# A two-block transformer kernel: split products of 512 and 256 columns become three of 256, and the weights' parts move by 192 bytes

## The chip, the core and the metric

The kernel runs on one core of a Trainium2 chip. The metric is the device time of one execution in microseconds (us); the time shown for the kernel before is the median of three runs. The profile is one execution of the same program, taken by the hardware profiler. Engines are named as the profile names them: PE (TensorE matmuls), PEld (TensorE weight loads), DVE (VectorE), ACT (ScalarE), POOL (GpSimd) and SP (SyncE, which issues the transfers).

## What is computed

Two transformer blocks work on one sequence of 256 tokens with 2,048 features, all in float32. Cut to the products that matter here:

```python
# first block: gated convolution mixer, then an MLP of width 8192
h = rms_norm(x) * (1 + sc1) + sh1
a, gt = split(h @ conv_w_in + b_in)            # 2048 -> 4096
u = silu(layer_norm(conv31(a * sigmoid(gt))))
x = x + (1 + g1) * (u @ conv_w_out + b_out)
h = rms_norm(x) * (1 + sc2) + sh2
x = x + (1 + g2) * (square(relu(h @ mlp_w1)) @ mlp_w2)
# second block: two kinds of attention, merged under gates, then a gated MLP of width 5632
h = rms_norm(x) * (1 + sc1) + sh1
qa, ka, va, qb, kb, vb, ga, gb = split(h @ w_in)
merged = sigmoid(ga) * (attn_a @ w_oa) + sigmoid(gb) * (attn_b @ w_ob)
x = x + g1 * (merged @ w_out)
h2 = rms_norm(x) * (1 + sc2) + sh2
x = x + g2 * ((silu(h2 @ w_gate) * (h2 @ w_up)) @ w_down)
return rms_norm(x)
```

## The kernel before

**Split products.** Activations are kept transposed: 16 blocks of 128 features (`KB`) by 256 tokens (`S`). Every weight matrix is cut into 128 x 128 blocks. To keep float32 accuracy with the faster `float32r` matmul, each operand is split into a high part and a low part (the rest of the value): an activation block lies in SBUF as high and low part side by side, 2 x 256 columns (tiles `hHL`, `uHL` and `m`); a weight block is split into `wh` and `wl`. Of the four products three are taken: high weight by high activation, high weight by low activation, low weight by high activation. We call these three products of one 128 x 128 weight block a unit; a product with K = 2,048 has 16 units.

`mm` (lines 184 to 207) makes a unit of two matmuls. `main` (L191) puts `wh` through the array against all 512 columns, high and low part in one go, and writes the 512 columns of a PSUM bank. `corr` (L194) puts `wl` against the 256 high columns and adds to the first half of the bank. So a finished product lies in two halves, and `total` (L238) adds them: ACT copies the second half to SBUF (L243), DVE adds the first half to it (L246). In the last unit `corr` comes first and `main` last.

`mm_one` (L208, matmul at L210) makes the same unit of three matmuls of 256 columns, all into the first half of the bank; nothing has to be added behind it. Before the change it serves the products of the convolution mixer (L755, L759, L828). The first six pairs of those products (`early`, L573) are also made of three matmuls of 256 columns.

Every matmul is issued with its own weight load (LDWEIGHTS); the load of the next matmul runs while one streams.

**Order.** `linear` (L222) goes through the output blocks of a matrix: for each it takes the next weights (`take`, L160), makes the product (`mm_group`, L214) and evicts it through a function of the stage (`ev_up`, `partial`, `residual`, `ev_qkv`, `ev_ff`). `take` keeps one weight tile ahead: a 1 MB transfer into `wf` (L169), then for each half an ACT cast to `wh` (L177) and a DVE subtraction to `wl` (L180). Between the steps small jobs run that make the modulation vectors (L263, L265, L286) from weights of their own. The engines' instructions keep the order of the program.

**Addresses.** The `big` pool gives each tag one place, one behind the other: `uHL` (also `front`), `hHL`, then `a1` (16 columns, 64 bytes a partition), then `m` (also `slots`, `room`, `att` and the accumulators `ya`); the pools with `wf`, `wh`, `wl` and the small tiles follow behind. In bytes modulo 256, `hHL` and `uHL` begin at 224, `m` at 32, and every `wh` and `wl` at 96; each block inside them lies a multiple of 512 bytes further on. So an activation lies 128 bytes past its weights modulo 256 where it is read from `hHL` or `uHL`, and 192 bytes where it is read from `m`.

Of the kernel before, what the change touches and what calls it, by code (L numbers as in the profile page):

```python
# [11 lines left out]
AF = mybir.ActivationFunctionType  # L12
# [3 lines left out]
P = 128  # L16
D = 2048
KB = D // P
S = 256
# [53 lines left out]
class Builder:  # L73
# [110 lines left out]
    def mm(self, ps, w, k, x, first, last):  # L184

        wh, wl = w[k // 8]
        h, l = wh[:, k % 8, :], wl[:, k % 8, :]
        full = x.rearrange("p a t -> p (a t)")

        def main():  # L190
            self.nc.tensor.matmul(ps, lhsT=h, rhs=full, start=first, stop=last, skip_group_check=True)  # L191

        def corr():
            self.nc.tensor.matmul(ps[:, :S], lhsT=l, rhs=x[:, 0, :], start=False, stop=False, skip_group_check=True)  # L194

        if last:
            corr()
            main()
        else:
            main()  # L200
            corr()

    def mm_one(self, w, x, nk):

        ps = self.mmps()
        for k in range(nk):
            wh, wl = w[k // 8]
            h, l = wh[:, k % 8, :], wl[:, k % 8, :]  # L208
            for i, (a, b) in enumerate(((h, 0), (h, 1), (l, 0))):
                self.nc.tensor.matmul(ps[:, :S], lhsT=a, rhs=x[:, k, b], start=(k == 0 and i == 0),  # L210
                                      stop=(k == nk - 1 and i == 2))
        return ps

    def mm_group(self, ws, x, ks, xs=None):  # L214

        xs = xs or ks
        pss = [self.mmps() for _ in ws]
        for i, (k, kx) in enumerate(zip(ks, xs)):
            for ps, w in zip(pss, ws):
                self.mm(ps, w, k, x[:, kx], i == 0, i == len(ks) - 1)  # L220
        return pss

    def linear(self, n, x, nk, evict, step=None, lead=3):

        j = 0
        while j < n:
# [6 lines left out]
                if step:  # L233
                    step()
            j += g

    def total(self, ps, bias=None, out=None):

        nc = self.nc
        tb = self.t1()  # L240
        s = self.t1() if out is None else out
        if bias is None:
            nc.scalar.copy(tb, ps[:, S:])  # L243
        else:
            nc.scalar.activation(tb, ps[:, S:], AF.Identity, bias=bias)
        nc.vector.tensor_tensor(out=s, in0=ps[:, :S], in1=tb, op=ALU.add)  # L246
        return s


    def mod_part(self, src, part, cvec, bias, out):  # L250
# [207 lines left out]
    def build(self):  # L458
# [44 lines left out]
        front = self.big.tile([P, 2 * KB * S], F32, tag="uHL", name="front")  # L503
        xn = front[:, :KB * S].rearrange("p (k t) -> p k t", t=S)
        h = self.actHL("hHL")
        a1 = self.keep([P, 16], "a1")
        slots = self.big.tile([P, 4, D], F32, tag="m", name="slots")
        ring = [slots[:, n] for n in range(4)]
        ring += [front[:, KB * S + n * D:KB * S + (n + 1) * D] for n in range(RING - 4)]
# [237 lines left out]
        for i in range(EARLY, KB):  # L747
            sg = self.t1()
            if i in NATIVE:

                ps = self.mmps()
                for k in range(KB):
                    nc.tensor.matmul(ps[:, :S], lhsT=w[:, k], rhs=xn[:, k], start=(k == 0), stop=(k == KB - 1))  # L753
            else:
                ps = self.mm_one(w, h, KB)  # L755
            w = self.take()
            turn()
            nc.scalar.activation(sg, ps[:, :S], AF.Sigmoid, bias=self.vec("conv_b_in", i + 16))
            ps = self.mm_one(w, h, KB)  # L759
            if i < KB - 1:  # L760
                w = self.take()
            turn()
            glu(i, ps[:, :S], sg)
# [27 lines left out]
                                 bias=self.vec("conv_ln_b", kb))  # L791
            self.split(s[:, kb, 0], s[:, kb, 1], t)

        def residual(j, ps, g, stat=None, part=None):

            if stat is not None and j == KB - 1:
                src = x[:, j]
                if part is not None:
                    src = part[:, j]
                    nc.vector.scalar_tensor_tensor(out=src, in0=src, scalar=g[:, j:j + 1], in1=x[:, j],  # L800
                                                   op0=ALU.mult, op1=ALU.add)
                t = self.t1()
                nc.vector.scalar_tensor_tensor(out=t, in0=ps[:, S:], scalar=g[:, j:j + 1], in1=src,
                                               op0=ALU.mult, op1=ALU.add)
                nc.vector.scalar_tensor_tensor(out=x[:, j], in0=ps[:, :S], scalar=g[:, j:j + 1], in1=t,
                                               op0=ALU.mult, op1=ALU.add)
                self.square_sum(stat, x[:, j], j)
                return
            t = self.total(ps)
            if part is not None:  # L810
                nc.vector.tensor_tensor(out=t, in0=t, in1=part[:, j], op=ALU.add)
            nc.vector.scalar_tensor_tensor(out=x[:, j], in0=t, scalar=g[:, j:j + 1], in1=x[:, j],
                                           op0=ALU.mult, op1=ALU.add)
            if stat is not None:
                self.square_sum(stat, x[:, j], j)

        def partial(j, ps, part, first):
            if first:
                self.total(ps, out=part[:, j])
            else:  # L820
                t = self.total(ps)
                nc.vector.tensor_tensor(out=part[:, j], in0=part[:, j], in1=t, op=ALU.add)

        g1 = self.keep([P, 16], "g1")
        nc.vector.tensor_scalar_add(g1, mod(0, G1), 1.0)
        st = self.aux()
        for j in range(16):
            ps = self.mm_one(self.take(), s, KB)  # L828
            t = self.t1()
            nc.scalar.activation(t, ps[:, :S], AF.Identity, bias=self.vec("conv_b_out", j))  # L830
            nc.vector.scalar_tensor_tensor(out=x[:, j], in0=t, scalar=g1[:, j:j + 1], in1=x[:, j],
                                           op0=ALU.mult, op1=ALU.add)
            self.square_sum(st[:, :S], x[:, j], j)
            self.step()
# [12 lines left out]
        for g in range(4):  # L847
            u = self.actHL("uHL")

            def ev_up(j, ps, u=u):  # L850
                t, r, v = self.total(ps), self.t1(), self.t1()
                nc.scalar.activation(r, t, AF.Relu)
                nc.scalar.activation(v, r, AF.Square)
                self.split(u[:, j, 0], u[:, j, 1], v)

            self.linear(16, h, KB, ev_up, step=self.step,
                        lead=3 if g == 0 else 1)
            if g < 3:
                self.linear(16, u, KB, lambda j, ps, g=g: partial(j, ps, ya, g == 0), step=self.step, lead=1)
            else:  # L860
                self.flush()
                nc.vector.tensor_scalar_add(g2, mod(0, G2), 1.0)
                self.linear(16, u, KB, lambda j, ps: residual(j, ps, g2, st[:, :S], ya), lead=1)
# [43 lines left out]
        def ev_qkv(j, ps):  # L907
            blk = QKV_ORDER[j]
            new = None
            if blk < 10:  # L910
                t = qg[:, blk] if blk < 8 else kv[:, blk - 8]
                self.total(ps, out=t)
                new = self.head_norm_rope(t, self.vec("q_norm_w_2" if blk < 8 else "k_norm_w_2"))
            elif blk < 12:
                new = value(self.total(ps), kv[:, blk - 8])
            elif blk < 28:
                n, i = (blk - 12) // 8, (blk - 12) % 8
                self.total(ps, out=qk[:, i % 2, n])
                if n:
                    new = gqa(i)  # L920
            else:
                new = nat(self.total(ps), blk - 28)
            self.advance()
            if new is not None:
                self.stages.append(new)
# [7 lines left out]
        def gates(j):  # L933
            out = []
            for b in (36 + j, 52 + j):
                g = self.t1()
                nc.scalar.activation(g, self.total(self.mm_group([self.take()], h, list(range(16)))[0]),
                                     AF.Sigmoid)
                out.append(g)
                self.advance()  # L940
            return out

        nxt = gates(0)
        for j in range(16):
# [3 lines left out]
            while self.stages:  # L948
                self.advance()
            w = self.take()  # L950
            oa = self.total(self.mm_group([w], y, list(range(8)))[0])
            nc.vector.tensor_tensor(out=sa, in0=sa, in1=oa, op=ALU.mult)
            ob = self.total(self.mm_group([w], y, list(range(8, 16)))[0])
            nc.vector.tensor_tensor(out=sb, in0=sb, in1=ob, op=ALU.mult)
            nc.vector.tensor_tensor(out=sa, in0=sa, in1=sb, op=ALU.add)
            self.split(m[:, j, 0], m[:, j, 1], sa)
# [17 lines left out]
        for gi, n in enumerate(FF_GROUPS):  # L974
# [1 line left out]
            tmp = {}  # L976

            def ev_ff(j, ps, u=u, tmp=tmp):
                t = self.total(ps)
                if j % 2 == 0:  # L980
                    g = self.t1()
                    nc.scalar.activation(g, t, AF.Silu)
                    tmp[j] = g
                else:
                    g = tmp.pop(j - 1)
                    v = self.t1()
                    nc.vector.tensor_tensor(out=v, in0=t, in1=g, op=ALU.mult)
                    self.split(u[:, j // 2, 0], u[:, j // 2, 1], v)

            self.linear(2 * n, h, KB, ev_ff,  # L990
# [129 lines left out]
```

## Time and profile before

| | |
|---|---|
| median of three runs | 2594.88 us (2594.2 to 2595.09) |
| profiled execution, its own time | 2594.32 us |
| its span, first to last instruction | 2592.5 us |
| mean granted TensorE clock | 0.989 |
| PE busy | 2527.7 us, 97% of the span, 15340 matmuls |
| PEld busy | 2164.4 us, 83% |
| DVE busy | 1828.1 us, 71% |
| ACT busy | 1323.5 us, 51% |
| moved by DMA | 638.43 MB, mean 246 GB/s |

Busy time is the time in which an engine had an instruction under way; matmuls overlap each other in the pipeline, so for PE the starts of successive matmuls tell more than the busy time does. The timeline view lists instructions by their start; the view of one source line gives the shortest, the median and the longest duration of its instructions.

### The profile page before, as it was taken

The numbers are of one execution on the slowest core, as the hardware profiler recorded it, in microseconds if no ns is written. First come the engines' busy times: TensorE is split into PE (matmuls) and PEld (weight loads), VectorE is DVE, ScalarE is ACT, GpSimd is POOL, SyncE is SP. The second block draws the span as 40 slices with busy tenths as digits, with TensorE's granted clock in tenths as the row PEclk, the third lists the DMA queues.
The fourth block names the chain that finished last, engine by engine and source line by source line (L and its number), as shares of the span: only waits on it lengthen the run. The fifth ranks groups of instructions, "written<-read, shape, count | busy, mean of one in ns | idle before, by whom it ended". The sixth has DMA issues, their size and how long they took to land.

```text
span 2592.5 us, 38179 instructions
## 1 busy us (share of the span) xinstructions
PE 2527.7 (97%) x15340; PEld 2164.4 (83%) x15340; DVE 1828.1 (71%) x2546; ACT 1323.5 (51%) x2143; POOL 152.1 (6%) x190
## 2 busy tenths in 40 slices
PE   6999899999999999999999999999999999999997
PEld 4788668788888888887888888888788888888886
DVE  4377754777887888867976778786766556666566
ACT  4367654554554644655454554554544444444454
POOL 0068800000000000000000000000000000000000
PEclk8999999999999999999999999999999999999999
DMA  9967478778888887854654677775466666665553
GB/s 394 416 242 279 180 274 313 277 279 318 297 291 292 296 293 289 313 190 168 227 202 167 209 251 267 275 271 191 160 222 228 222 209 229 216 223 203 187 176 116
DMA packets 110338, 638.43 MB, mean 246 GB/s; under 512 B 16336, under 2 KB 16592, under 8 KB 51792
## 3 DMA queue, kind: packets, MB, share of 16 engines
q1 hardware_dynamic: 110160, 635.99, 68.7%
q8 instruction: 120, 1.97, 0.3%
q14 instruction: 58, 0.48, 0.0%
HBM read 633.85 MB, written 2.10 MB: 245 GB/s over the span
## 4 chain that ended last, share of the span: by engine, by line
PE 95%; DMA 2%; DVE 1%; ACT 1%; issue 0%; POOL 0%; SPq 0%; DVEq 0%; ACTq 0%; POOLq 0%
PE mm L191 51%; PE mm L194 27%; PE mm L210 8%; PE aux L286 2%; PE mm L573 2%; DMA slots<-in_mod_a_dram 1%; PE mm L753 1%; PE aux L530 1%; DMA front<-in_mod_a_dram 1%; PE aux L369 1%; PE mm L639 1%; PE aux L422 1%; PE aux L454 1%; PE aux L271 0%; PE aux L573 0%; DMA x<-in_xT_dram 0%
## 5 line engine op out<-in xcount | busy, mean ns | idle before, releaser
L191 PE MATMUL mm<-hHL,wh 128*128 128x512 f32 x3520 | 1243.1, 397 | 11.9 <-DVE hHL L380 11.9
L180 DVE TENSOR_TENSOR wl<-wf,wh 128x1024 fp32r<-128x1024 f32 (+1 forms) x794 | 965.9, 1219 | 356.5 <-ACT wh L177 333.6
L177 ACT CAST wh<-wf 128x1024 fp32r<-128x1024 f32 (+1 forms) x794 | 825.4, 1042 | 404.8 <-PE mm L191 240.1
L194 PE MATMUL mm<-hHL,wl 128*128 128x256 f32 x3520 | 960.9, 283 | 0.6 <-DVE wl L180 0.6
L191 PEld LDWEIGHTS mm<-hHL,wh 128*128 128x128 f32 x3520 | 652.6, 188 | 149.6 <-issue 8.9
L191 PE MATMUL mm<-uHL,wh 128*128 128x512 f32 x1984 | 691.4, 394 | 0.0
L194 PEld LDWEIGHTS mm<-hHL,wl 128*128 128x128 f32 x3520 | 663.7, 189 | 20.5 <-DVE wl L180 1.2
L194 PE MATMUL mm<-uHL,wl 128*128 128x256 f32 x1984 | 536.1, 282 | 0.0
L243 ACT COPY t<-mm 128x256 f32<-128x256 f32 x377 | 140.5, 373 | 588.2 <-PE mm L191 586.2
L191 PEld LDWEIGHTS mm<-uHL,wh 128*128 128x128 f32 x1984 | 364.5, 188 | 73.9
L194 PEld LDWEIGHTS mm<-uHL,wl 128*128 128x128 f32 x1984 | 372.9, 188 | 13.4
L265 DVE SCALAR_TENSOR_TENSOR acc<-wm,silu_c,acc 128x1024 f32<-128x1024 f32 x210 | 268.8, 1280 | 30.7 <-DMA wm<-in_w_ada_dram 26.9
L246 DVE TENSOR_TENSOR t<-mm,t 128x256 f32<-128x256 f32 x319 | 134.9, 423 | 181.1 <-ACT t L243 180.5
L655 POOL TENSOR_TENSOR room<-room,front 128x255 f32<-128x255 f32 (+9 forms) x180 | 146.6, 815 | 171.4 <-ACT front L654 158.4
L210 PE MATMUL mm<-hHL,wh 128*128 128x256 f32 x544 | 99.9, 286 | 0.0
L210 PE MATMUL mm<-uHL,wh 128*128 128x256 f32 x512 | 96.2, 288 | 0.7 <-DVE uHL L133 0.7
L210 PEld LDWEIGHTS mm<-uHL,wh 128*128 128x128 f32 x512 | 79.8, 191 | 16.4 <-issue 11.7
L210 PEld LDWEIGHTS mm<-hHL,wh 128*128 128x128 f32 x544 | 84.0, 189 | 6.9 <-issue 4.5
L191 PE MATMUL mm<-m,wh 128*128 128x512 f32 x256 | 89.5, 397 | 0.0
L665 DVE SCALAR_TENSOR_TENSOR mm<-room,vecs,mm 128x255 f32<-128x255 f32 (+9 forms) x180 | 84.7, 471 | 4.8
L654 ACT ACTIVATE front<-room,vecs 128x255 f32<-128x255 f32 (+9 forms) x180 | 74.7, 487 | 7.9 <-POOL room L655 7.9
L210 PE MATMUL mm<-hHL,wl 128*128 128x256 f32 x272 | 76.7, 282 | 0.0
(174 smaller groups left out, 1776.1 us busy)
## 6 DMA issues: line engine op xcount, KB each, us to landing
wf<-in_w_dram SPq DMA_DIRECT2D x128, 1024.0 KB, 6.7
wm<-in_w_ada_dram SPq DMA_DIRECT2D x96, 1024.0 KB, 5.2
wf<-in_win_dram SPq DMA_DIRECT2D x68, 1024.0 KB, 5.0
wm<-in_mod_w_dram SPq DMA_DIRECT2D x64, 1024.0 KB, 5.8
wf<-in_wg_dram SPq DMA_DIRECT2D x44, 1024.0 KB, 5.0
wf<-in_wu_dram SPq DMA_DIRECT2D x44, 1024.0 KB, 4.8
wf<-in_wd_dram SPq DMA_DIRECT2D x32, 896.0 KB, 4.6
slots<-in_mod_a_dram SPq DMA_DIRECT2D x22, 1024.0 KB, 15.0
```

The lines of the kernel that those rows point to most:

```text
L177: self.nc.scalar.copy(wh, w[:, k0:k0 + n, :])
L180: self.nc.vector.tensor_tensor(out=wl, in0=w[:, k0:k0 + n, :], in1=wh, op=ALU.subtract)
L191: self.nc.tensor.matmul(ps, lhsT=h, rhs=full, start=first, stop=last, skip_group_check=True)
L194: self.nc.tensor.matmul(ps[:, :S], lhsT=l, rhs=x[:, 0, :], start=False, stop=False, skip_group_check=True)
L210: self.nc.tensor.matmul(ps[:, :S], lhsT=a, rhs=x[:, k, b], start=(k == 0 and i == 0), stop=(k == nk - 1 and i == 2))
L243: nc.scalar.copy(tb, ps[:, S:])
L246: nc.vector.tensor_tensor(out=s, in0=ps[:, :S], in1=tb, op=ALU.add)
L265: nc.vector.scalar_tensor_tensor(out=acc, in0=w[:, i], scalar=cvec[:, k + i:k + i + 1], in1=acc, op0=ALU.mult, op1=ALU.add)
L286: nc.tensor.matmul(row[32 * j:32 * j + 32, :], lhsT=cpad[:, k], rhs=w[:, j * 512:(j + 1) * 512], start=(k == 0), stop=(k == KB - 1), skip_ ...
L654: nc.scalar.activation(pr, u[:, PAD:PAD + S - s], AF.Identity, scale=tap(i, j))
L655: nc.gpsimd.tensor_tensor(out=dst[:, s:], in0=dst[:, s:], in1=pr, op=ALU.add)
L665: nc.vector.scalar_tensor_tensor(out=acc[:, s:], in0=u[:, PAD:PAD + S - s], scalar=tap(i, j), in1=acc[:, s:], op0=ALU.mult, op1=ALU.add)
```

## The change

A unit is now always three matmuls of 256 columns, high by high, high by low, low by high, into one half of a bank. `mm_one` and `total` are gone; products are read from PSUM by whatever instruction uses them first. `a1` is allocated 64 columns wide, of which 16 are used.

```diff
         wh, wl = w[k // 8]
         h, l = wh[:, k % 8, :], wl[:, k % 8, :]
-        full = x.rearrange("p a t -> p (a t)")
-        def main():
-            self.nc.tensor.matmul(ps, lhsT=h, rhs=full, start=first, stop=last, skip_group_check=True)
-        def corr():
-            self.nc.tensor.matmul(ps[:, :S], lhsT=l, rhs=x[:, 0, :], start=False, stop=False, skip_group_check=True)
...
+        for i, (a, b) in enumerate(((h, 0), (h, 1), (l, 0))):
+            self.nc.tensor.matmul(ps, lhsT=a, rhs=x[:, b], start=(first and i == 0), stop=(last and i == 2))
...
-        pss = [self.mmps() for _ in ws]
+        pss = [self.mmps()[:, :S] for _ in ws]
...
-    def total(self, ps, bias=None, out=None):
...
-        a1 = self.keep([P, 16], "a1")
+        a1 = self.keep([P, 64], "a1")[:, :16]
...
-                ps = self.mm_one(w, h, KB)
+                ps = self.mm_group([w], h, range(KB))[0]
...
-        def residual(j, ps, g, stat=None, part=None):
-            if stat is not None and j == KB - 1:
...
+        def residual(j, ps, g, stat, part=None):
+            src = x[:, j]
+            if part is not None:
+                src = part[:, j]
+                nc.vector.scalar_tensor_tensor(out=src, in0=src, scalar=g[:, j:j + 1], in1=x[:, j],
                                                op0=ALU.mult, op1=ALU.add)
+            nc.vector.scalar_tensor_tensor(out=x[:, j], in0=ps, scalar=g[:, j:j + 1], in1=src,
                                            op0=ALU.mult, op1=ALU.add)
+            self.square_sum(stat, x[:, j], j)
 
         def partial(j, ps, part, first):
             if first:
-                self.total(ps, out=part[:, j])
+                nc.scalar.copy(part[:, j], ps)
             else:
-                t = self.total(ps)
-                nc.vector.tensor_tensor(out=part[:, j], in0=part[:, j], in1=t, op=ALU.add)
+                nc.vector.tensor_tensor(out=part[:, j], in0=part[:, j], in1=ps, op=ALU.add)
...
-                t, r, v = self.total(ps), self.t1(), self.t1()
-                nc.scalar.activation(r, t, AF.Relu)
+                r, v = self.t1(), self.t1()
+                nc.scalar.activation(r, ps, AF.Relu)
```

The other evictions (`ev_qkv`, `gates`, the merge, `ev_ff`) lose their `total` in the same way: a plain ACT copy, an activation, or a DVE product reads the bank. With `a1` 192 bytes longer, everything behind it moves by 192 bytes: `m` then begins at 224 modulo 256 and every `wh` and `wl` at 32, while `hHL` and `uHL` stay at 224. Every activation then lies 192 bytes past its weights' parts modulo 256.

On PE, in a product of the second block's input projection (`mm` is the PSUM tile, `hHL` the activations, `wh` and `wl` the weights' parts), the order was, to the end of the product:

```order
L191 MATMUL mm_12454<-hHL_11569,wh_12383 128x512
L194 MATMUL mm_12454<-hHL_11569,wl_12384 128x256
L191 MATMUL mm_12454<-hHL_11569,wh_12383 128x512
L194 MATMUL mm_12454<-hHL_11569,wl_12384 128x256 x2
L191 MATMUL mm_12454<-hHL_11569,wh_12383 128x512
```

and in such a product after the change, where the second half of the weights begins:

```order
L189 MATMUL mm_13861<-hHL_13139,wh_13766 128x256 x2
L189 MATMUL mm_13861<-hHL_13139,wl_13767 128x256
L189 MATMUL mm_13861<-hHL_13139,wh_13770 128x256 x2
L189 MATMUL mm_13861<-hHL_13139,wl_13771 128x256
L189 MATMUL mm_13861<-hHL_13139,wh_13770 128x256 x2
```

Each unit has three matmuls in place of two, and so three weight loads in place of two.

On ACT, around the eviction of an up product of the first block's MLP (`t` are small tiles, `wf` the loaded weights), before:

```order
L177 CAST wh_10685<-wf_10683 128x1024
L243 COPY t_1600_10660<-mm_10627 128x256
L177 CAST wh_10689<-wf_10683 128x1024
L852 ACTIVATE t_1602_10664<-t_1601_10661 128x256
L853 ACTIVATE t_1603_10665<-t_1602_10664 128x256
L132 CAST uHL_9825<-t_1603_10665 128x256
```

and after:

```order
L177 CAST wh_12115<-wf_12113 128x1024
L177 CAST wh_12119<-wf_12113 128x1024
L805 ACTIVATE t_1406_12106<-mm_12057 128x256
L806 ACTIVATE t_1407_12107<-t_1406_12106 128x256
L132 CAST uHL_11009<-t_1407_12107 128x256
```

The copy out of PSUM is gone, and the first activation reads the bank itself.

## Rows read from the trace of the kernel before

**Rows 1.** Page, parts 1 and 4: busy us by engine; the chain that ended last.

```profile
PE 2527.7 (97%) x15340; PEld 2164.4 (83%) x15340; DVE 1828.1 (71%) x2546; ACT 1323.5 (51%) x2143; POOL 152.1 (6%) x190
...
PE 95%; DMA 2%; DVE 1%; ACT 1%; issue 0%; POOL 0%; SPq 0%; DVEq 0%; ACTq 0%; POOLq 0%
PE mm L191 51%; PE mm L194 27%; PE mm L210 8%; PE aux L286 2%; PE mm L573 2%; DMA slots<-in_mod_a_dram 1%; PE mm L753 1%; PE aux L530 1%; DMA front<-in_mod_a_dram 1%; PE aux L369 1%; PE mm L639 1%; PE aux L422 1%; PE aux L454 1%; PE aux L271 0%; PE aux L573 0%; DMA x<-in_xT_dram 0%
```

**Rows 2.** Groups by line: out<-in xcount | busy us, mean ns | idle before, releaser.

```profile
L191 PE MATMUL mm<-hHL,wh 128*128 128x512 f32 x3520 | 1243.1, 397 | 11.9 <-DVE hHL L380 11.9
L191 PE MATMUL mm<-uHL,wh 128*128 128x512 f32 x1984 | 691.4, 394 | 0.0
L243 ACT COPY t<-mm 128x256 f32<-128x256 f32 x377 | 140.5, 373 | 588.2 <-PE mm L191 586.2 <-DVE t L342 1.9
L246 DVE TENSOR_TENSOR t<-mm,t 128x256 f32<-128x256 f32 x319 | 134.9, 423 | 181.1 <-ACT t L243 180.5
L210 PE MATMUL mm<-hHL,wh 128*128 128x256 f32 x544 | 99.9, 286 | 0.0
L210 PE MATMUL mm<-uHL,wh 128*128 128x256 f32 x512 | 96.2, 288 | 0.7 <-DVE uHL L133 0.7
L191 PE MATMUL mm<-m,wh 128*128 128x512 f32 x256 | 89.5, 397 | 0.0
```

**Rows 3.** Timeline of PE in an up product (offset 128): start us, us, instruction.

```profile
501.24 0.39 PE L191 MATMUL mm<-hHL,wh 128*128 128x512 f32 x1
501.48 0.28 PE L194 MATMUL mm<-hHL,wl 128*128 128x256 f32 x1
...
505.80 0.40 PE L191 MATMUL mm<-hHL,wh 128*128 128x512 f32 x1
```

**Rows 4.** Timeline of PE in an output product of the second block (from `m`, offset 192).

```profile
1765.20 0.40 PE L191 MATMUL mm<-m,wh 128*128 128x512 f32 x1
...
1768.03 0.40 PE L191 MATMUL mm<-m,wh 128*128 128x512 f32 x1
```

**Rows 5.** Timeline of PE in three products of 256 columns a matmul (offset 128).

```profile
149.08 0.40 PE L210 MATMUL mm<-hHL,wh 128*128 128x256 f32 x2
149.32 0.28 PE L210 MATMUL mm<-hHL,wl 128*128 128x256 f32 x1
...
152.29 0.40 PE L210 MATMUL mm<-hHL,wh 128*128 128x256 f32 x2
...
275.19 0.40 PE L210 MATMUL mm<-hHL,wh 128*128 128x256 f32 x2
...
280.23 0.40 PE L210 MATMUL mm<-hHL,wh 128*128 128x256 f32 x2
...
417.00 0.39 PE L210 MATMUL mm<-uHL,wh 128*128 128x256 f32 x2
...
421.98 0.40 PE L210 MATMUL mm<-uHL,wh 128*128 128x256 f32 x2
```

**Rows 6.** Timeline of PE behind the second norm, where the clock is low.

```profile
1207.60 0.63 PE L191 MATMUL mm<-hHL,wh 128*128 128x512 f32 x1
...
1210.80 0.63 PE L191 MATMUL mm<-hHL,wh 128*128 128x512 f32 x1
```

**Rows 7.** Stretches: us, busy us (instructions) PE, PEld, DVE, ACT, POOL, PEclk, DMA share, GB/s.

```profile
1206.20:1211.20 5.00, 5.00 (x15) 4.26 (x16) 5.00 (x14) 2.61 (x6) 0.00 (x0) 0.50 0.12 49
501.00:506.00 5.00, 5.00 (x30) 4.39 (x29) 3.20 (x5) 3.51 (x6) 0.00 (x0) 1.00 0.81 272
26.00:140.00 114.00, 108.64 (x856) 86.58 (x857) 44.92 (x81) 47.85 (x70) 0.00 (x0) 0.94 0.95 388
491.00:1208.00 717.00, 712.03 (x4069) 622.54 (x4068) 567.76 (x684) 377.56 (x587) 0.00 (x0) 1.00 0.78 279
```

**Rows 8.** Lines L210 and L191: durations, shortest/median/longest ns, first and last start us.

```profile
L210 PE MATMUL mm<-hHL,wh x544: 274/282/471, 140.1 to 294.6; 128*128 128x256 f32 x182
L210 PE MATMUL mm<-hHL,wl x272: 278/281/287, 140.3 to 294.7; 128*128 128x256 f32 x136
...
L191 PE MATMUL mm<-m,wh x256: 389/397/483, 1734.8 to 1825.6; 128*128 128x512 f32 x128
...
L191 PE MATMUL mm<-uHL,wh x1: 398/398/398, 2578.3 to 2578.3; 128*128 128x512 f32 x1
```

**Rows 9.** Timeline of DVE behind the last matmul of the last product.

```profile
2578.78 0.48 DVE L803 SCALAR_TENSOR_TENSOR t<-mm,mods,ya 128x256 f32<-128x256 f32 x1 [2.90 <-PE mm L191]
2579.30 0.48 DVE L805 SCALAR_TENSOR_TENSOR x<-mm,mods,t 128x256 f32<-128x256 f32 x1
```

More of the change, by code (lines that the diff above doesn't have):

```diff
@@ L187, in mm @@
         h, l = wh[:, k % 8, :], wl[:, k % 8, :]
-        full = x.rearrange("p a t -> p (a t)")
-        def main():
-            self.nc.tensor.matmul(ps, lhsT=h, rhs=full, start=first, stop=last, skip_group_check=True)
-        def corr():
-            self.nc.tensor.matmul(ps[:, :S], lhsT=l, rhs=x[:, 0, :], start=False, stop=False, skip_group_check=True)
[L196 to L212, printed above, removed]
+        for i, (a, b) in enumerate(((h, 0), (h, 1), (l, 0))):
+            self.nc.tensor.matmul(ps, lhsT=a, rhs=x[:, b], start=(first and i == 0), stop=(last and i == 2))
     def mm_group(self, ws, x, ks, xs=None):
         xs = xs or ks
-        pss = [self.mmps() for _ in ws]
+        pss = [self.mmps()[:, :S] for _ in ws]
         for i, (k, kx) in enumerate(zip(ks, xs)):
@@ L235, in linear @@
             j += g
-    def total(self, ps, bias=None, out=None):
[L239 to L247, printed above, removed]
     def mod_part(self, src, part, cvec, bias, out):
@@ L758, in build @@
             nc.scalar.activation(sg, ps[:, :S], AF.Sigmoid, bias=self.vec("conv_b_in", i + 16))
-            ps = self.mm_one(w, h, KB)
+            ps = self.mm_group([w], h, range(KB))[0]
             if i < KB - 1:
@@ L792, in build @@
             self.split(s[:, kb, 0], s[:, kb, 1], t)
-        def residual(j, ps, g, stat=None, part=None):
-            if stat is not None and j == KB - 1:
[L797 to L803, printed above, removed]
-                                               op0=ALU.mult, op1=ALU.add)
[L805 to L808, printed above, removed]
-            t = self.total(ps)
-            if part is not None:
-                nc.vector.tensor_tensor(out=t, in0=t, in1=part[:, j], op=ALU.add)
-            nc.vector.scalar_tensor_tensor(out=x[:, j], in0=t, scalar=g[:, j:j + 1], in1=x[:, j],
+        def residual(j, ps, g, stat, part=None):
[3 more added lines that the diff above has]
+                nc.vector.scalar_tensor_tensor(out=src, in0=src, scalar=g[:, j:j + 1], in1=x[:, j],
+                                               op0=ALU.mult, op1=ALU.add)
+            nc.vector.scalar_tensor_tensor(out=x[:, j], in0=ps, scalar=g[:, j:j + 1], in1=src,
                                            op0=ALU.mult, op1=ALU.add)
-            if stat is not None:
-                self.square_sum(stat, x[:, j], j)
+            self.square_sum(stat, x[:, j], j)
         def partial(j, ps, part, first):
             if first:
-                self.total(ps, out=part[:, j])
+                nc.scalar.copy(part[:, j], ps)
             else:
-                t = self.total(ps)
-                nc.vector.tensor_tensor(out=part[:, j], in0=part[:, j], in1=t, op=ALU.add)
+                nc.vector.tensor_tensor(out=part[:, j], in0=part[:, j], in1=ps, op=ALU.add)
         g1 = self.keep([P, 16], "g1")
@@ L827, in build @@
         for j in range(16):
-            ps = self.mm_one(self.take(), s, KB)
+            ps = self.mm_group([self.take()], s, range(KB))[0]
             t = self.t1()
@@ L911, in ev_qkv @@
                 t = qg[:, blk] if blk < 8 else kv[:, blk - 8]
-                self.total(ps, out=t)
+                nc.scalar.copy(t, ps)
                 new = self.head_norm_rope(t, self.vec("q_norm_w_2" if blk < 8 else "k_norm_w_2"))
             elif blk < 12:
-                new = value(self.total(ps), kv[:, blk - 8])
+                t = self.t1()
+                nc.scalar.copy(t, ps)
+                new = value(t, kv[:, blk - 8])
             elif blk < 28:
                 n, i = (blk - 12) // 8, (blk - 12) % 8
-                self.total(ps, out=qk[:, i % 2, n])
+                nc.scalar.copy(qk[:, i % 2, n], ps)
                 if n:
@@ L921, in ev_qkv @@
             else:
-                new = nat(self.total(ps), blk - 28)
+                t = self.t1()
+                nc.scalar.copy(t, ps)
+                new = nat(t, blk - 28)
             self.advance()
@@ L936, in gates @@
                 g = self.t1()
-                nc.scalar.activation(g, self.total(self.mm_group([self.take()], h, list(range(16)))[0]),
-                                     AF.Sigmoid)
+                nc.scalar.activation(g, self.mm_group([self.take()], h, range(16))[0], AF.Sigmoid)
                 out.append(g)
@@ L950, in build @@
             w = self.take()
-            oa = self.total(self.mm_group([w], y, list(range(8)))[0])
+            oa = self.mm_group([w], y, range(8))[0]
             nc.vector.tensor_tensor(out=sa, in0=sa, in1=oa, op=ALU.mult)
-            ob = self.total(self.mm_group([w], y, list(range(8, 16)))[0])
+            ob = self.mm_group([w], y, range(8, 16))[0]
             nc.vector.tensor_tensor(out=sb, in0=sb, in1=ob, op=ALU.mult)
@@ L978, in ev_ff @@
             def ev_ff(j, ps, u=u, tmp=tmp):
-                t = self.total(ps)
                 if j % 2 == 0:
                     g = self.t1()
-                    nc.scalar.activation(g, t, AF.Silu)
+                    nc.scalar.activation(g, ps, AF.Silu)
                     tmp[j] = g
@@ L986, in ev_ff @@
                     v = self.t1()
-                    nc.vector.tensor_tensor(out=v, in0=t, in1=g, op=ALU.mult)
+                    nc.vector.tensor_tensor(out=v, in0=ps, in1=g, op=ALU.mult)
                     self.split(u[:, j // 2, 0], u[:, j // 2, 1], v)
```

## Prediction

> **What bounds the kernel now.** I read the chain that ended last first: 95% of it is PE, and 78% the two lines of the split product [rows 1]. The groups then show that nothing holds PE up there: 11.9 us of idle time stand before 5,760 matmuls of L191, while the copies of L243 wait 586 us for PE [rows 2]. So the spacing of matmuls sets the time, and I read that from starts, since durations overlap.
>
> The unit as it is: from 501.24 to 505.80 lie 13 units, 4.56 us, or **351 ns** each [rows 3]. Fed from `m`, where the offset is already 192, 8 units take 2.83 us, 354 ns [rows 4]. Where the unit is already made of three matmuls, 9 units take 3.21 us and 14 take 4.98 us, 357 and 356 ns; in one slow product 14 take 5.04 us, 360 ns [rows 5]. I use **356.5 ns**. All these are at the full clock (1.00, 2.4 GHz); behind the second norm the clock is 0.50 (1.2 GHz), and there 5 units take 3.20 us, 640 ns [rows 6, 7]. Half of that would be 320 ns. So at the full clock some 31 ns of the unit of two, and 36 ns of the unit of three, are not columns passing through but something that doesn't scale with the clock. In the unit of three that loss is not the same for each matmul: durations of one form, at one offset, go from 274 to 287 ns around a median of 281 or 282 [rows 8]. A matmul of the median length stands for a spacing of 356.5 / 3 = 119 ns, so duration less 163 ns is the spacing: 278 ns stands for 115 and 274 for 111.
>
> **The change, part by part.** The base is the profiled execution, 2594.3 us, 0.6 us under the median of the runs.
>
> 1. *5,760 units (3,520 + 1,984 + 256 [rows 2]) go from two matmuls to three, at offset 192.* No row shows three matmuls at 192, so this price is bounded from both sides: 320 ns if the loss goes altogether [rows 6], 360 ns if it stays at its worst [rows 5]. I take the loss for a collision of two reads of SBUF, the moving activations and the next matmul's weights, that hits some matmuls and misses others. For it: it is absent at half speed, and it varies at fixed addresses and a fixed amount of work. If so, the relative place of the two streams decides, and that is what the longer `a1` sets anew. A matmul that is missed needs 115 ns by the 278 of [rows 8], which lies between the bounds and is a value seen in this form; three give 345 ns. That is 6 ns a unit: 5,760 x 6 = **-34.6 us**.
> 2. *The units that were of three already.* 544 and 512 matmuls on `wh`, two to a unit, are 528 units [rows 2]; 356.5 to 345 gives **-6.1 us**. The 192 early units (L573) I cost at nothing: between 26 and 140 us the DMA is 0.95 busy and the chain runs through its transfers [rows 1, 7]. If that cover were gone it would be 2 us more.
> 3. *377 ACT copies of 373 ns and as many DVE additions of 423 ns go* (319 of them in one row), 300 us of engine time in all [rows 2]. I cost this at nothing: PE doesn't wait for an eviction in the long stages, and PE's stream hides both engines with or without them. Nothing new is queued behind the direct reads that wasn't queued behind the copy: they wait for the same last matmul.
> 4. *Three ends.* Behind the last product of three stages PE waits for a norm. There two DVE instructions of 0.48 us followed the last matmul [rows 9]; now one does, since the other no longer needs the product. Three times 0.5 us: **-1.5 us**.
> 5. *Transfers.* The weights are the same. In the busiest long stage the DMA is 0.78 busy [rows 7]; a PE that is 2% faster asks for 0.80. Nothing.
>
> Sum: 34.6 + 6.1 + 1.5 = 42 us less: **2552 us**.
>
> **Weighed against a rule.** The loss varies from one matmul to the next and vanishes at half speed [rows 6, 8], which a plain cost per instruction would not. The Trainium skill, "TensorE: Matmul & The Clock Gate", section "Wait — 56ns, not 53.3ns?", has such a cost: at the full clock each back-to-back matmul adds about 2.5 ns to its columns, whatever its addresses. By it one more matmul a unit would make the kernel an estimated 5,760 x 2.5 ns = 14 us slower. It speaks against this change, though the trace differs: it loses 31 ns in a unit of two where that rule allows 5 [rows 3, 6].
>
> **The rivals.**
>
> *Addresses mean nothing; the third matmul costs what it costs at L210.* Then each unit goes from 351 to 356.5 ns: 5,760 x 5.5 = +31.7, less 1.5 us: **2624 us**, slower; at the worst spacing, 360 ns, +51.8 + 1.8 - 1.5 gives 2646. It decides if three matmuls take over 351 ns, 117 each. For it: units from `m` are at 192 already and are no quicker (354 against 351 ns) [rows 3, 4]; and the very last matmul of 512 columns, with no load beside it (PE has nothing more to do until the norm), takes 398 ns, like the median 397 of those from `m` [rows 8]. So at least for 512 columns some of the loss isn't the load's. Against it: the spread of L210 at one offset, and that those two rows are of another form. The Trainium skill, "SBUF — State Buffer", section "Who interferes with whom", says that PE has two independent read ports, one for moving data and one for weights, and never waits on anyone. By that rule offsets can't matter, and this rival holds; the trace of before settles it neither way.
>
> *The loss goes nearly altogether.* At the shortest duration seen, 274 ns, the spacing is 111 ns and the unit 333: 5,760 x 18 = -103.7, 528 x 23.5 = -12.4, and -1.5 us: **2477 us**; at the floor of 320 ns, -178.6 - 19.3 - 1.5: 2395. For it: the half-speed row. Against it: no stretch at the full clock runs so.
>
> *Gain and price cancel.* At 117 ns a matmul the unit stays at 351; only the old units of three (528 x 5.5 = 2.9 us) and the ends gain: **2590 us**. A few tenths of a ns either side keep it within 0.2%, 5 us, which is about what a measurement of this kernel can tell from no change.
>
> That the layout isn't as described is excluded: places follow from the sizes of the tiles in one pool.
>
> **How the numbers follow.** The forecast's case (112 to 116.5 ns a matmul) gets 0.38, the loss gone 0.19, cancelling 0.12, addresses without effect 0.31. Faster: 0.38 + 0.19 = 0.57; within 0.2%: 0.12; slower: 0.31. The bounds of part 1 are far apart, so the range must reach both the good end and the L210 price: 2480 leaves out most of the loss gone (0.13), and 2630 the slow spacing (0.07). The likeliest case alone would lie between 2500 and 2587.
>
> **What would show it.** In the profile after, successive starts of a long product (now at L189) should lie 345 ns a unit apart, with durations of 278 ns or less as the rule and little spread, alike from `hHL`, `uHL` and `m`. Medians of 281 or 282 ns and 356 ns a unit would prove the first rival; 272 to 274 the second. PE's idle time should stay near 65 us (the span of 2592.5 less 2527.7 [rows 1]), with DVE and ACT some 160 and 140 us less busy; if PE waited for evictions instead, part 3 would be wrong. One `residual` instruction should stand behind each stage's last matmul. If the time falls while the spacing doesn't, my reasons are wrong whatever the number.

## The result, and the profile after

The changed kernel takes **2559.86 us** (median of 4 runs, 2536.55 to 2576.23) where the kernel before takes 2594.99 us (4 runs, 2594.2 to 2596.12). The ratio is **0.9835**, 95% interval 0.9804 to 0.9866. The forecast was 2552 us in a range of 2480 to 2630. The ratio leaves out the run of 2576.23 us, which counts as slow for lying over 1.5% above the fastest, though its granted clock (0.989) is that of the others; the two medians, 35.1 us apart, give 0.986. One thing was not forecast at all: the runs of the changed kernel lie 1.6% apart, those of the kernel before 0.07%. The profiled execution is the fastest run, 2536.55 us, its granted clock 0.990.

First the page, part 1: busy us by engine, share of the span of 2534.8 us.

```profile
PE 2469.6 (97%) x21100; PEld 2362.7 (93%) x21100; DVE 1683.3 (66%) x2166; ACT 1227.1 (48%) x1834; POOL 152.1 (6%) x190
```

PE has 5,760 more matmuls than in [rows 1] and is busy 58.1 us less; its idle time is 2534.8 less 2469.6 = 65.2 us, as before (64.8). So nearly all of the 57.7 us by which the span is shorter came out of the spacing of matmuls. Where, the view of the product's line shows (shortest/median/longest ns, first and last start us):

```profile
L189 PE MATMUL mm<-hHL,wh x7584: 275/276/582, 138.8 to 2444.3; 128*128 128x256 f32 x200
...
L189 PE MATMUL mm<-uHL,wh x4480: 276/276/582, 338.7 to 2521.2; 128*128 128x256 f32 x195
...
L189 PE MATMUL mm<-m,wh x512: 276/276/467, 1702.9 to 1790.9; 128*128 128x256 f32 x171
```

The median is 276 ns, where three-matmul units had 281 and 282 in [rows 8]. Against the starts in [rows 8], the part from the first long product to the first product from `m` shrank from 1594.7 to 1564.1 us (-30.6), the part from there to the last product from 843.5 to 818.3 us (-25.2); the front gave 1.3 us and the end 0.6.

The timeline of PE in an MLP product of the first block, as in [rows 3], has 17 units between these two starts:

```profile
779.90 0.39 PE L189 MATMUL mm<-uHL,wh 128*128 128x256 f32 x2
...
785.68 0.39 PE L189 MATMUL mm<-uHL,wh 128*128 128x256 f32 x2
```

5.78 us, **340 ns a unit**, 113.3 a matmul. But earlier in the same execution 15 units take 5.31 us:

```profile
500.06 0.40 PE L189 MATMUL mm<-hHL,wh 128*128 128x256 f32 x2
...
505.37 0.40 PE L189 MATMUL mm<-hHL,wh 128*128 128x256 f32 x2
```

That is 354 ns. The two stretches have the same form, the same offset and the same granted clock (1.00). I call them the fast and the slow pattern. At the low clock the unit still takes 640 ns (here 3 units in 1.92 us), as in [rows 6]:

```profile
1182.21 0.63 PE L189 MATMUL mm<-hHL,wh 128*128 128x256 f32 x2
...
1184.13 0.63 PE L189 MATMUL mm<-hHL,wh 128*128 128x256 f32 x2
```

And behind the last matmul DVE now has one instruction before the norm, where [rows 9] have two:

```profile
2521.65 0.48 DVE L767 SCALAR_TENSOR_TENSOR x<-mm,mods,ya 128x256 f32<-128x256 f32 x1 [4.17 <-PE mm L189]
```

From its start to the end of the span are 13.15 us, before 13.72 (2592.5 less 2578.78): 0.57 us less.

### The profile page after: what moved, and what is told of

It reads as the page before. It is cut to its first block, busy times and chain, and to the rows that moved or that the text cites. A ratio compares the mean times of both kernels' runs of the same rounds, so it can differ in the third digit from the quotient of the medians.

```text
span 2534.8 us, 49435 instructions
## 1 busy us (share of the span) xinstructions
PE 2469.6 (97%) x21100; PEld 2362.7 (93%) x21100; DVE 1683.3 (66%) x2166; ACT 1227.1 (48%) x1834; POOL 152.1 (6%) x190
## 5 line engine op out<-in xcount | busy, mean ns | idle before, releaser
L189 PE MATMUL mm<-hHL,wh 128*128 128x256 f32 x7584 | 1323.9, 279 | 8.8 <-ACT hHL L344 7.7
L180 DVE TENSOR_TENSOR wl<-wf,wh 128x1024 fp32r<-128x1024 f32 (+1 forms) x794 | 965.8, 1221 | 539.2 <-ACT wh L177 523.8
L189 PEld LDWEIGHTS mm<-hHL,wh 128*128 128x128 f32 x7584 | 1154.2, 189 | 20.5 <-ACT hHL L344 8.9
L189 PE MATMUL mm<-uHL,wh 128*128 128x256 f32 x4480 | 772.3, 278 | 1.4 <-DVE uHL L133 0.7
L189 PEld LDWEIGHTS mm<-hHL,wl 128*128 128x128 f32 x3792 | 716.3, 189 | 1.2 <-DVE wl L180 0.8
L189 PEld LDWEIGHTS mm<-uHL,wh 128*128 128x128 f32 x4480 | 677.2, 188 | 17.4 <-issue 12.6
L189 PE MATMUL mm<-uHL,wl 128*128 128x256 f32 x2240 | 619.6, 277 | 0.0
L189 PE MATMUL mm<-m,wh 128*128 128x256 f32 x512 | 87.6, 277 | 0.0
L189 PEld LDWEIGHTS mm<-m,wh 128*128 128x128 f32 x512 | 77.4, 188 | 0.0
L189 PE MATMUL mm<-m,wl 128*128 128x256 f32 x256 | 70.7, 276 | 0.0
L539 PE MATMUL mm<-hHL,wh 128*128 128x256 f32 x320 | 62.5, 296 | 3.4 <-ACT hHL L132 3.4
L539 PEld LDWEIGHTS mm<-hHL,wh 128*128 128x128 f32 x320 | 51.9, 199 | 9.9 <-issue 6.1
L251 PE MATMUL aux<-wm,cpad 128*32 128x512 f32 x384 | 53.9, 610 | 4.5 <-DMA wm<-in_mod_w_dram 4.5
```

The source lines that it names most:

```text
L180: self.nc.vector.tensor_tensor(out=wl, in0=w[:, k0:k0 + n, :], in1=wh, op=ALU.subtract)
L189: self.nc.tensor.matmul(ps, lhsT=a, rhs=x[:, b], start=(first and i == 0), stop=(last and i == 2))
L251: nc.tensor.matmul(row[32 * j:32 * j + 32, :], lhsT=cpad[:, k], rhs=w[:, j * 512:(j + 1) * 512], start=(k == 0), stop=(k == KB - 1), skip_ ...
L539: nc.tensor.matmul(dst, lhsT=w[:, c, kk], rhs=h[:, k, b], start=(k == 0 and n == 0 and half == 0), stop=(k == KB - 1 and n == 2 and half = ...
```

## Experiments

The theory to be tested is the forecast's: the relative place of activations and weights' parts modulo 256 bytes sets the spacing, by a collision of the moving read with the next matmul's weight load. The main rival is that addresses mean nothing and the form alone gains. The four kernels of one group below ran on one chip, with runs of the kernel before beside them (2594.59, 2595.34 and 2594.87 us).

### The form without the place, and the place without the form

**e1** takes the changed kernel and puts `a1` back:

```diff
-        a1 = self.keep([P, 64], "a1")[:, :16]
+        a1 = self.keep([P, 16], "a1")
```

> The changed kernel with a1 at 16 columns again: three matmuls of 256 a unit, activations from hHL and uHL 128 bytes past the weights' parts, those from m at 192 as ever. Offset theory (the forecast's): 356.5 ns a unit as at L210 of before, medians 281 to 282 ns, 2615 to 2630 us; units from m (192 here too) stay at the 340 to 343 ns of the changed kernel. Rival, addresses mean nothing and the form alone gains: 340 to 350 ns a unit everywhere, 2540 to 2575 us as the changed kernel.

Measured 2618.94 us, ratio 1.0098 (1.0083 to 1.0114): **slower than the kernel before**. The timeline of PE, first in a product from `hHL` (offset 128), then in one from `m` (192):

```profile
499.83 0.40 PE L189 MATMUL mm<-hHL,wh 128*128 128x256 f32 x2
...
505.88 0.40 PE L189 MATMUL mm<-hHL,wh 128*128 128x256 f32 x2
...
1799.89 0.39 PE L189 MATMUL mm<-m,wh 128*128 128x256 f32 x2
...
1805.67 0.39 PE L189 MATMUL mm<-m,wh 128*128 128x256 f32 x2
```

17 units take 6.05 us (356 ns) from `hHL` and 5.78 us (340 ns) from `m`. Within one execution, with one form and one place of the weights, the two stretches differ by 16 ns a unit. The rows of `m` alone would prove little, since in other runs below `m`, at 192 as well, takes 353 or 354 ns. But from `hHL` and `uHL` no eight units in a row of this trace take under 354 ns each, where the changed kernel has 340 over most of its length, and `hHL` lies where it lay there: only what stands behind it has moved. That ends the rival.

**e2** gives the kernel before the longer `a1`, and nothing else:

```diff
-        a1 = self.keep([P, 16], "a1")
+        a1 = self.keep([P, 64], "a1")[:, :16]
```

> The kernel before with a1 at 64 columns: 512+256 a unit, all offsets 192. Offset theory as I applied it to the pair of matmuls only through m's rows: the unit from hHL goes from 351 to the 353 or 354 ns that m has, so 5,504 x 2 = 11 us slower; the 528 old units of three gain 6 to 8 us; in all 2590 to 2605 us. A rival by which 192 is simply the good place for any form: 340 to 346 ns a unit, 2540 to 2570 us. Addresses mean nothing: 2594 to 2596 us.

Measured 2599.67 us, ratio 1.0019 (1.0011 to 1.0028): also slower, as the rows of `m` had said. PE's timeline in a product of 512 + 256 columns (18 units), then in one that always had three matmuls (8 units):

```profile
799.61 0.40 PE L191 MATMUL mm<-uHL,wh 128*128 128x512 f32 x1
...
805.96 0.40 PE L191 MATMUL mm<-uHL,wh 128*128 128x512 f32 x1
```

```profile
201.72 0.39 PE L210 MATMUL mm<-hHL,wh 128*128 128x256 f32 x2
...
204.44 0.39 PE L210 MATMUL mm<-hHL,wh 128*128 128x256 f32 x2
```

353 ns for the first, 340 for the second. So each half of the change alone costs time, the form 24 us and the place 5; together they gain 35. In these two runs the fast pattern shows only where both meet.

### Is it the place in 64 bytes?

Every activation row of 1,024 bytes begins at 32 modulo 64, and I suspected a 64-byte piece too many. **e3** moves everything from `hHL` on by 32 bytes; **e4** does it with `a1` at 16 columns too:

```diff
-        sel = self.keep([P, 1], "sel")
+        sel = self.keep([P, 16], "sel")[:, :1]
```

> The changed kernel with sel at 16 columns, so that hHL, uHL and m begin at 0 modulo 256 (before: 224) and the weights' parts at 64: the offset stays 192, but each row of 1,024 bytes now begins at a multiple of 64. Offset theory alone: as the changed kernel, 340 to 350 ns a unit, 2536 to 2577 us. Rival, the moving operand is read in pieces of 64 bytes and a row that begins at 32 modulo 64 touches one piece more (17 for 16, about 6 per cent): 320 to 327 ns a unit, 2430 to 2470 us.

> As the run before with a1 at 16 columns: rows begin at multiples of 64, activations of hHL and uHL 128 bytes past the weights' parts, those of m 192. Offset theory alone: 356.5 ns a unit from hHL and uHL, 2615 to 2630 us, m 340 to 350. Pieces of 64 bytes alone: 320 to 327 ns a unit everywhere, 2430 to 2470 us. Addresses mean nothing: 2540 to 2575.

e3 took 2535.36 us (2533.05 to 2545.5), ratio 0.978 (0.9764 to 0.9796); e4 2618.2 us, 1.0097 (1.0083 to 1.011). e3's timeline has 17 units in 5.78 us again, 340 ns and not 325:

```profile
800.06 0.39 PE L189 MATMUL mm<-uHL,wh 128*128 128x256 f32 x2
...
805.84 0.39 PE L189 MATMUL mm<-uHL,wh 128*128 128x256 f32 x2
```

The idea of pieces falls; both kernels stand where their offset puts them. One control in e4 missed: products from `m`, at 192, ran in the slow pattern there (354 ns), and so they did in e5 and e7 below.

### Other offsets

**e5 to e8** change the one number in the length of `a1`: 32, 48, 56 and 72 columns in place of 64.

> The changed kernel with a1 at 32 columns: hHL and uHL 64 bytes past the weights' parts modulo 256, m at 192 as ever. If the offset counts modulo 128 (two halves that the reads take in turn), 64 is as good as 192: 340 to 350 ns a unit, 2535 to 2577 us. If 192 alone is good: 356 ns, 2615 to 2625 us. m, the control: 340 to 353 ns either way.

> The changed kernel with a1 at 48 columns: hHL and uHL at the weights' own place modulo 256, m at 192. If the offset counts modulo 128, 0 is as 128: 356 ns a unit, 2615 to 2625 us. If nearness of the two reads makes the collision: worse than 128, 358 to 365 ns, 2630 to 2680 us. If 128 alone is bad: 340 to 350 ns, 2535 to 2577.

> The changed kernel with a1 at 56 columns: hHL and uHL 224 bytes past the weights' parts, which now begin at a multiple of 64 while the activations don't. If steps of 64 bytes are what counts, 224 is as one of its neighbours 192 (340 to 350 ns, 2535 to 2577 us) or 0; if each 32 bytes count, a value between, 343 to 356 ns, 2545 to 2620 us.

> The changed kernel with a1 at 72 columns: hHL and uHL 160 bytes past the weights' parts, between the bad 128 (356 ns) and the good 192 (340 to 350 ns). Steps of 64 bytes: as one of the two, 2535 to 2577 or 2615 to 2625 us; each 32 bytes: between, 343 to 356 ns, 2545 to 2620 us.

| offset of `hHL`, `uHL` | time, us | ratio to before, 95% | unit, ns |
|---|---|---|---|
| 0 (e6) | 2642.37 | 1.0181 (1.0165 to 1.0196) | 360 |
| 64 (e5) | 2604.71 | 1.0032 (1.0019 to 1.0044) | 354, and 340 in one long stretch |
| 128 (e1) | 2618.94 | 1.0098 (1.0083 to 1.0114) | 356 |
| 160 (e8) | 2604.49 | 1.0034 (1.0021 to 1.0047) | 353 and 360 |
| 192 (the change) | 2559.86 | 0.9835 (0.9804 to 0.9866) | 340 and 354 |
| 224 (e7) | 2612.58 | 1.0067 (1.0052 to 1.0082) | 355 |

The worst, offset 0, has 17 units in 6.12 us:

```profile
499.73 0.40 PE L189 MATMUL mm<-hHL,wh 128*128 128x256 f32 x2
...
505.85 0.40 PE L189 MATMUL mm<-hHL,wh 128*128 128x256 f32 x2
```

Of the six offsets tried only 192 is faster than the kernel before. 0 isn't like 128 (360 and 356 ns), so the offset doesn't count modulo 128; 160 and 224 aren't like 192, so steps of 32 bytes count. But 64 has the two patterns of 192. e5's timeline shows 16 units in 5.44 us and, later, 16 in 5.66:

```profile
499.94 0.39 PE L189 MATMUL mm<-hHL,wh 128*128 128x256 f32 x2
...
505.38 0.39 PE L189 MATMUL mm<-hHL,wh 128*128 128x256 f32 x2
...
700.21 0.40 PE L189 MATMUL mm<-hHL,wh 128*128 128x256 f32 x2
...
705.87 0.40 PE L189 MATMUL mm<-hHL,wh 128*128 128x256 f32 x2
```

These are 340 and 354 ns again. The fast stretch ends at 546 us, and almost everything else in that run is slow. So what sets 64 apart from 192 is not the price of either pattern but how seldom the fast one came. At the other four offsets no eight units in a row from `hHL` or `uHL` took under 350 ns each. That two reads at one place (offset 0) are worst agrees with a collision but doesn't prove one.

### Does each weight load collide by itself?

**e11** puts 64 bytes between the places of `wh` and `wl`, so that activations lie 192 past `wh` and 128 past `wl`; **e12** is the mirror, 128 past `wh` and 192 past `wl`, for `hHL` and `uHL`. The three matmuls stand on three lines in both (L194 and L195 with `wh` by the high and the low part, L196 with `wl`):

```diff
+            self.gap()
             wl = self.sp.tile([P, n, P], F32R, tag="wl", name=self.nm("wl"))
...
+    def gap(self):
+        if not self.gapped:
+            self.gapped = self.sp.tile([P, 16], F32, tag="gap", bufs=1, name="gap")
+            self.nc.vector.memset(self.gapped, 0.0)
```

(In e12 the gap is 48 columns and `a1` is 16.)

> The changed kernel with 64 bytes put between the places of wh and of wl, and the three matmuls on three lines: activations of hHL, uHL (and m) lie 192 bytes past wh as before, but 128 past wl. Collision of a matmul's read with the next matmul's weight load: the loads of wl run beside the second matmul (wh by the low activations), so that is the one whose durations grow from 276 to 280 or more, the other two stay at 276; a third of the loss, 345 ns a unit, 2555 to 2580 us. If a matmul is slowed by its own weights: the third line grows instead. If the two parts' places don't act by themselves: 2536 to 2577 us with all three lines alike.

> The mirror of it: a1 at 16 columns, so that activations of hHL and uHL lie 128 past wh, and 192 bytes between wh and wl, so that they lie 192 past wl. Collision with the next load: the first and third matmul grow, whose neighbours are loads of wh, the second stays at 276 ns; two thirds of the loss, 351 ns a unit, 2580 to 2605 us. Own weights: the first and second grow. No separate action: 356 ns, 2615 to 2625 us.

e11 took 2613.04 us, ratio 1.007 (1.0057 to 1.0083); e12 2616.59 us, 1.0086 (1.0073 to 1.0099). The durations by line in e11:

```profile
L194 PE MATMUL mm<-hHL,wh x3792: 276/283/580, 139.7 to 2518.4; 128*128 128x256 f32 x200
...
L195 PE MATMUL mm<-hHL,wh x3792: 276/282/583, 139.8 to 2518.6; 128*128 128x256 f32 x200
...
L196 PE MATMUL mm<-hHL,wl x3792: 274/280/467, 139.9 to 2518.7; 128*128 128x256 f32 x200
```

I had forecast 345 ns a unit, with L195 alone grown. Instead all three lines grew, L194 most, and 17 units take 6.02 us, 354 ns:

```profile
499.75 0.28 PE L194 MATMUL mm<-hHL,wh 128*128 128x256 f32 x1
...
505.77 0.28 PE L194 MATMUL mm<-hHL,wh 128*128 128x256 f32 x1
```

One part of the two at another place costs nearly as much as both (356 ns in e1). None of the three cases that I had set down for e11 came true, and e12's time is that of its third case, no separate action: the loss is not a price for each matmul with a badly placed neighbour, added up. As far as these two runs show, it belongs to the sequence as a whole, which either runs at 340 ns or doesn't.

### Why do the runs differ?

**e9** is the changed kernel again, **e10** is e3 again, on one chip.

> The changed kernel itself once more, for its spread. If each undisturbed run of matmuls falls by chance into one of two patterns, 340 ns a unit or about 350, and keeps it to the next break, runs differ by some 10 to 30 us again, between 2536 and 2577 us, and the profile shows another mix of the two over the stretches than before. If the slow stretches belong to certain stages of the program: the same stretches are slow again, those from 470 to 570 and from 1290 to 1530 us, and the spread must have another cause.

> The kernel with sel at 16 columns once more (rows at multiples of 64, offset 192), on the same chip as the run of the changed kernel. If rows at multiples of 64 keep PE in the fast pattern: 2533 to 2546 us again, below the changed kernel with an interval that leaves it out. If its first four runs were luck: medians within 15 us of the changed kernel and the same spread, 2533 to 2577.

e9 took 2566.0 us (6 runs, 2547.17 to 2576.5), ratio 0.9876 (0.9843 to 0.9909); e10 2537.33 us (5 runs, 2530.62 to 2546.8), 0.9769 (0.9757 to 0.9782). e9's profiled run took 2570.21 us, and its timeline shows the patterns the other way round, 16 units in 5.44 us where the first profile was slow, 15 in 5.30 us late in the program:

```profile
499.91 0.39 PE L189 MATMUL mm<-hHL,wh 128*128 128x256 f32 x2
...
505.35 0.39 PE L189 MATMUL mm<-hHL,wh 128*128 128x256 f32 x2
...
1900.02 0.40 PE L189 MATMUL mm<-hHL,wh 128*128 128x256 f32 x2
...
1905.32 0.40 PE L189 MATMUL mm<-hHL,wh 128*128 128x256 f32 x2
```

340 and 353 ns. Two rows of its product line give the length of the part from `m` on:

```profile
L189 PE MATMUL mm<-uHL,wh x4480: 275/276/582, 340.1 to 2554.9; 128*128 128x256 f32 x195
...
L189 PE MATMUL mm<-m,wh x512: 276/281/469, 1706.9 to 1798.0; 128*128 128x256 f32 x171
```

2554.9 less 1706.9 is 848.0 us against 818.3 in the first profile: 29.7 of the 33.6 us between the two spans. That part has 2,368 units (256 from `m`, 1,408 up and gate, 704 down); 13.3 ns for each would be 31.6. So the spread is the share of time in the slow pattern. What decides between the two is not settled. In the four profiled runs with all at 192 (the change, e3, e9, e10), a fast stretch of the long stages stayed fast across the eight small matmuls of L236 that interrupt it, while a slow one stayed slow or became fast there. e10 shows a change, with the starts of units before and after:

```profile
2109.52 0.40 PE L189 MATMUL mm<-hHL,wh 128*128 128x256 f32 x2
...
2109.88 0.40 PE L189 MATMUL mm<-hHL,wh 128*128 128x256 f32 x2
...
2110.24 1.04 PE L236 MATMUL aux<-const,acc 128*128 128x128 f32 x8
2111.03 0.48 PE L189 MATMUL mm<-hHL,wh 128*128 128x256 f32 x2
...
2111.47 0.39 PE L189 MATMUL mm<-hHL,wh 128*128 128x256 f32 x2
...
2111.81 0.39 PE L189 MATMUL mm<-hHL,wh 128*128 128x256 f32 x2
```

0.36 us a unit before L236, 0.34 after it. Back to slow it went across the norms and the convolution's and attention's short products, and in the long stages where PE had waited for an operand. The slow stretch that ends above began so, behind a `wl` that DVE finished (L180) at 1809.50 us; its matmul starts at 1809.56, the next one 0.22 us later:

```profile
1807.97 0.39 PE L189 MATMUL mm<-hHL,wh 128*128 128x256 f32 x2
...
1808.28 1.22 DVE L180 TENSOR_TENSOR wl<-wf,wh 128x1024 fp32r<-128x1024 f32 x1
...
1809.33 0.39 PE L189 MATMUL mm<-hHL,wh 128*128 128x256 f32 x2
...
1809.56 0.39 PE L189 MATMUL mm<-hHL,wl 128*128 128x256 f32 x1
...
1809.78 0.40 PE L189 MATMUL mm<-hHL,wh 128*128 128x256 f32 x2
...
1810.84 0.40 PE L189 MATMUL mm<-hHL,wh 128*128 128x256 f32 x2
```

Four units take 340 ns each before it, three take 353 behind it. The same wait in the first profile of the changed kernel (DVE done at 1810.58 us) left the fast pattern standing, with 11 units in 3.74 us, 340 ns:

```profile
1810.64 0.38 PE L189 MATMUL mm<-hHL,wl 128*128 128x256 f32 x1
...
1811.21 0.39 PE L189 MATMUL mm<-hHL,wh 128*128 128x256 f32 x2
...
1814.95 0.39 PE L189 MATMUL mm<-hHL,wh 128*128 128x256 f32 x2
```

So a wait can be where the pattern changes, but it doesn't fix which one follows. e9's second half stayed slow to the end. Not all of it is chance, perhaps: the stretch around 1500 us was slow in all four.

**The fastest version** is e10 (and e3): its interval leaves out that of the changed kernel on the same chip, and its nine runs in two sets lie between 2530.62 and 2546.8 us, against 2536.55 to 2576.5 for ten of the changed kernel. Why 32 bytes more make the slow pattern rarer was not shown.

## Why the prediction was right, and where it wasn't

**What bounds the kernel** held. The saving is PE's; its idle time stayed at 65 us with the copies and additions gone.

**Part 1**, the forecast's term of -34.6 us, was right in sign and nearly in size, and half right in its reason. That the place decides was right: e1 is 2618.94 us, close to the 2624 that the first rival gave for three matmuls at the old price, and e2 is where the rows of `m` put it. So the choice to leave [rows 4] aside as "of another form" was sound: at 192, 512 + 256 gains nothing and three of 256 do. But no stretch of the changed kernel runs at 345 ns a unit. That is a mean between 340 and 353: the median run is 23.3 us longer than the profiled one, 3.7 ns for each of 6,288 units. That the median came within 8 us of the forecast is thus in part luck, of how the two patterns were mixed in those runs; e5, with the same two prices and little of the fast one, takes 2604.71 us. I had read the spread of durations in [rows 8] as some matmuls hit by a collision and others missed; the step "A matmul that is missed needs 115 ns" fails, since the fast stretches have 113.3, and e11 and e12 take the picture of single collisions away. "Little spread" and "alike from `hHL`, `uHL` and `m`" came true for the durations of the profiled run, not for every run.

For the median run, 35.1 us were gained; less the 6.1 and 1.5 us that I gave to the next two parts, 27.5 us are left for 5,760 units, 4.8 ns each where I had 6.

**Part 2** has the right mechanism: in e2 the old units of three go from 356.5 to 340 ns in the stretch shown, and stay at 353 in some other products. It was not measured apart over all 528.

**Part 3**, nothing for the evictions, held by PE's idle time. Its check was off on ACT: 140 us less busy were forecast, 96.4 came. 68 of the 377 copies stay as copies (rows below), 24.6 us. The rest lies in overlap, which busy time counts once: the durations of all of ACT's instructions add up to 1424.5 us before and 1303.5 after, 121.0 less.

```profile
L773 ACT COPY ya<-mm 128x256 f32<-128x256 f32 x32 | 11.6, 363 | 0.0
...
L873 ACT COPY att<-mm 128x256 f32<-128x256 f32 x16 | 5.8, 365 | 0.0
L865 ACT COPY att<-mm 128x256 f32<-128x256 f32 x10 | 3.6, 367 | 0.0
L878 ACT COPY t<-mm 128x256 f32<-128x256 f32 x8 | 2.9, 366 | 0.0
...
L869 ACT COPY t<-mm 128x256 f32<-128x256 f32 x2 | 0.7, 373 | 0.0
```

DVE is 144.8 us less busy, for 160 forecast; its durations add up to 159.3 us less. **Part 4**: 0.57 us at the last end, for 0.5.

**The rules weighed.** In e1 products of one form run at 340 and 356 ns a unit, with the moving data at another place and the weights at the same. The statement of the Trainium skill, "SBUF — State Buffer", section "Who interferes with whom", that PE has two independent read ports and never waits on anyone, would leave no room for that; here the measurement decides. And a matmul of 256 columns costs 320 / 3 = 106.7 ns by half the low clock's time, so the fast pattern adds 6.7 ns and the worst offset 13.3 ns. The fixed 2.5 ns of the Trainium skill, "TensorE: Matmul & The Clock Gate", section "Wait — 56ns, not 53.3ns?", is too small for every stretch shown here at the full clock. That the loss vanishes at the low clock, which the prediction held against that rule, doesn't speak against it: the section has the cost at the full clock alone.

**What stays open**: what the two reads share, why the fast pattern is common at 192, rare at 64 and was not seen at the other offsets, and what decides between the two. A collision of moving reads and weight loads is argued, not shown: no kernel without the weight loads was tried.

## To carry to other kernels

Where a kernel's bound is the spacing of small matmuls, treat the place of the moving operand relative to the weights modulo 256 bytes as a parameter, try it in steps of 32 bytes by lengthening a small tile, and judge form and place together: here each alone made the kernel slower and both together some 1.3% faster (the mean of ten runs of the changed kernel is 2560.9 us). The gain hangs on how much of a run is in the fast pattern: at 353 ns the new unit is dearer than the old one of 351. A tile of another length put anywhere in front undoes it unseen, so fix the places once a good one is found. Where runs spread after such a change and didn't before, compare the spacing in the same stretch of two profiled runs before taking a median for the price of an instruction.

## What the hardware showed beside that

Three steady unit times of three matmuls fall on a grid with the low clock's 640 halved: 320, 340, 353.3 and 360 ns are 48, 51, 53 and 54 times 6.67 ns. The 356 of offset 128 does not; it is a mean of units that differ. In the long stages a pattern, once taken, can hold for hundreds of microseconds: e10 is slow from 1809.78 to 2110.24 us.

ACT read a finished product from PSUM faster than from SBUF. The groups by line of ACT, the first of the kernel before, the second of the changed one (busy us, mean ns):

```profile
L852 ACT ACTIVATE t<-t 128x256 f32<-128x256 f32 x64 | 26.8, 418 | 17.6 <-DVE t L246 17.4
```

```profile
L805 ACT ACTIVATE t<-mm 128x256 f32<-128x256 f32 x64 | 24.0, 375 | 0.0
```

The same 64 activations take 418 ns out of SBUF and 375 out of PSUM.
